# One float32 matmul per product in place of three fp32r matmuls, in a hybrid encoder block on one core

## The chip, the core and the metric

One core of a Trainium2 chip runs the whole block in one launch. The metric is the device time of one execution in microseconds. TensorE (PE) multiplies, with its weight loads shown apart (PEld); VectorE (DVE), ScalarE (ACT) and GpSimd (POOL) work beside it; SyncE (SP) issues most DMAs. Weights and activations are float32 in memory and must come out with float32 accuracy.

## The reference, cut to what matters

```python
x = x + 0.5 * swiglu(rms_norm(x, ffn1_norm), w_gate1, w_up1, w_down1)     # 2048 -> 5504 -> 2048
proj = rms_norm(x, mix_norm) @ w_in                                       # 2048 -> 11280
(gq, gk, gv, gz, ga, gb, aq, ak, av, gate_gdn, gate_att) = split(proj)
o_gdn = gdn_branch(gq, gk, gv, gz, ga, gb, ...)     # conv, chunked gated delta rule, 8 heads of 128
o_att = chunk_attention_branch(aq, ak, av, ...)     # banded softmax attention, 8 heads of 128
m = sigmoid(gate_gdn) * (o_gdn @ w_branch_gdn) + sigmoid(gate_att) * (o_att @ w_branch_att)
x = x + m @ w_out
x = x + 0.5 * swiglu(rms_norm(x, ffn2_norm), w_gate2, w_up2, w_down2)
```

There are 256 tokens, batch 1, one layer, all in float32. Nearly all work is in the large matrix products: 256 tokens times some 100 million weights, read once.

## The kernel before, in words

**Tiles.** The 256 tokens are two halves of 128. An activation block is a 128 x 128 tile (128 features on the partitions, 128 tokens), held as the stationary operand; the weights are the moving operand, up to 512 columns wide, and a result bank is 128 tokens x 512 columns in PSUM. There are 4 result banks of the kind `acc` and 4 of the kind `core`.

**Three matmuls per product.** Every operand of a large product is split in two numbers that TensorE takes in the type fp32r: the high part is the value cast to fp32r (ScalarE), the low part is the value less the high part (VectorE). `product` (lines 507 to 509) adds high x high, high x low and low x high into the same bank. Activations are split by `Xr.plain`, `Xr.more`, `split_to` and `bank_sums`, weights by `split` and `prepare`.

**Seven products in place of eight.** For chosen pairs of k tiles and pairs of column groups (`fast` pairs, in `seven`) the 2 x 2 blocks are multiplied by Winograd's form of Strassen's scheme: seven products of 128 x 128 times 128 x 512 in place of eight. The weights' four sums (`s`, lines 430 to 432) are made on VectorE, and the activations' sums by `act_sums`. The products go to eight banks, whose contents are put together on VectorE and ScalarE (lines 593 to 597, 610). Other pairs use eight plain products. Lists such as `FAST`, `FOUR`, `MIX`, `DOWN`, `DEEP` and `LAST` say which pairs are fast in which product.

**The weights' way.** `plan` lists all weight items in the order of use: one item is two DMAs of 512 KB, a pair of k tiles for two column groups. `load` issues the DMAs of an item to a tile `raw` on SyncE, `split` makes the casts and sums, `prepare` the low halves, and `take_weights` hands the parts to the products. `LOAD` = 2 items are loaded ahead of the one being split, `PREP` = 5 products or rows are ready ahead of TensorE. All of these tiles are in a pool `heap` of 22 buffers of 8 KB per partition. A plain item uses three of them (`raw`, `wh`, `wl`), a fast one five (`raw`, `s`, `w`, `sh`, `sl`) and a half-size one (`v`).

**Order of the work.** The first FFN, the input projections, attention woven with the projections for the gated delta rule (`weave`), the delta rule woven with branch and gate products, the merge, the output product and the second FFN follow each other. `after(n, f)` puts small work n weight items later; `issue_after` places chosen instructions behind others in the order of issue. The second FFN ends in `seven(..., late=...)`, where the last pair's products alternate with the transposes of finished output parts (`store`), and the last column group is transposed and stored after it.

**Other matmuls.** 163 small matmuls (attention scores and values, the delta rule) take plain float32 operands already, at 8 to 256 columns, and 501 are transposes of 128 x 128 tiles; the change leaves them as they are.

Of the kernel before, what the change touches and what calls it, by code (L numbers as in the profile page):

```python
# [12 lines left out]
F32R = mybir.dt.float32r  # L13
# [23 lines left out]
TAIL = {"1": ((0, 1, 2, 3, 4, 5), (0, 1, 5, 3, 4, 2)), "2": ((0, 1, 2, 3, 4, 5), (0, 1, 5, 3, 4, 2))}  # L37
APART = (0, 1, 2, 4, 3, 7, 5, 6)
FIRST = (1, 0, 3, 2, 5, 4, 7, 6)
QUAD = {2: (0, 0), 3: (1, 0), 4: (0, 1), 8: (1, 1)}  # L40
STAND = (3, 4, 6, 7)
CHUNKS = ((0, 4), (4, 8), (8, 11))
# [5 lines left out]
def block_kernel(ctx: ExitStack, tc: tile.TileContext, a: dict, out: bass.AP):  # L48
# [26 lines left out]

    def f32(ap):
        return ap.bitcast(F32)
# [54 lines left out]
    def split_to(hi, lo, src):  # L132
        nc.scalar.copy(hi, src)
        nc.vector.tensor_sub(lo, src, f32(hi))  # L134
# [20 lines left out]
    class Xr:  # L155
# [4 lines left out]
        def __init__(self, nm, wi, fast=()):  # L160
            self.nm, self.wi, self.fast = nm, wi, fast
            self.blk, self.half = {}, None
            self.acc = sp.tile([P, 2, 4], F32, name=f"ssq{nm}", tag="ssq", bufs=2)
            self.rn = sp.tile([P, 2], F32, name=f"rn{nm}", tag="rn", bufs=2)
            self.half_rn = sp.tile([P, 2], F32, name=f"rh{nm}", tag="rh", bufs=2)

        def place(self, j):
            if j in self.fast:
                self.blk[j] = heap([P, 2, 8, P], F32R, f"xf{self.nm}_{j}")
            elif self.half is None:  # L170
                self.half = heap([P, 2, 2, 4, P], F32R, f"xr{self.nm}_{j}")
                self.blk[j] = self.half[:, 0]
            else:
                self.blk[j], self.half = self.half[:, 1], None
            return self.blk[j]
# [4 lines left out]
        def plain(self, j, src, later=None):  # L180

            b = self.place(j)
            for i in range(2):
                hi, lo = (b[:, s, 2 * i : 2 * i + 2, :].rearrange("p t x -> p (t x)") for s in range(2))
                nc.scalar.activation(hi, src(i), AF.Copy, scale=self.w(j, i))
                low = lambda i=i, hi=hi, lo=lo: nc.vector.scalar_tensor_tensor(
                    lo, src(i), self.w(j, i), f32(hi), op0=ALU.mult, op1=ALU.subtract
                )
                later.append(low) if later is not None else low()

        def scale(self, j, src, a):
            for i in range(2):
                nc.scalar.activation(
                    a[:, 2 * i : 2 * i + 2, :].rearrange("p t x -> p (t x)"), src(i), AF.Copy, scale=self.w(j, i)
                )

        def more(self, j, src, blocks=slice(4, 8)):

            a, s = (wide(f"x{x}{self.nm}{j}").rearrange("p (b x) -> p b x", x=P) for x in "as")
            self.scale(j, src, a)  # L200
            act_sums([a[:, b] for b in range(4)], s)
            for b, v in ((0, a), (4, s)):
                if b >= blocks.start:
                    split_to(self.blk[j][:, 0, b : b + 4], self.blk[j][:, 1, b : b + 4], v)

        def add(self, j, src):
            if j in self.fast:
                self.place(j)
                self.more(j, src, slice(0, 8))
            else:  # L210
                self.plain(j, src)
# [20 lines left out]
        def sums_of(self, j, i):  # L232
            return [self.blk[j][:, s, i] for s in range(2)]

        def more_again(self, pairs):

            sums = {}
            for i, j in enumerate(pairs):
                if i % 2 == 0:
                    tile = heap([P, 2, 2, 4, P], F32R, f"xm{self.nm}{j}_{taken[0]}")  # L240
                sums[j] = tile[:, i % 2]

            def make(j):
                a, s = (wide(f"m{x}{self.nm}{j}").rearrange("p (b x) -> p b x", x=P) for x in "as")
                nc.vector.tensor_add(a, f32(self.blk[j][:, 0]), f32(self.blk[j][:, 1]))
                act_sums([a[:, b] for b in range(4)], s)
                split_to(sums[j][:, 0], sums[j][:, 1], s)

            for i, j in enumerate(pairs):
                after(2 + 2 * i, lambda j=j: make(j))  # L250
            return lambda j, b: self.sums_of(j, b) if b < 4 else [sums[j][:, s, b - 4] for s in range(2)]
# [4 lines left out]
    def quads(blk):  # L256
        return lambda k, t: [blk[k // 4][:, k % 4, s, t * P : (t + 1) * P] for s in range(2)]
# [59 lines left out]
    def mixing():  # L317
# [16 lines left out]
        yield from sevens(*gates[0:2])  # L334
        yield from sevens(*gates[2:4])
# [7 lines left out]
    PREP, LOAD = 5, 2  # L343
# [30 lines left out]
    def begin():  # L374
# [5 lines left out]
        with ExitStack() as order:  # L380
            for ins in copied:
                order.enter_context(tc.issue_after(ins))
            if loaded[0][0] - 1 in range(1, 8):
                order.enter_context(tc.issue_after(casts[loaded[0][0] - 1].ins))
            split(*loaded.popleft())
            copied.clear()

    def split(i, fast, pieces, raw):

        if i in (2, 3, 5, 6, 7, 8):  # L390
            j = FIRST[i if i < 4 else i - 1]
            xr1.plain(j, pair_of_x(j), lows)
        if not fast:
            out = []
            ms = [n * kk * (P if len(src.shape) == 3 else 1) for src, n, kk in pieces]
            cuts = [(slice(0, 2), ms[0])] if ms[0] == ms[1] else [(slice(at, at + 1), m) for at, m in enumerate(ms)]
            hl = [heap([P, 2, 1024], F32R, f"w{x}{i}") for x in "hl"]
            if i < 4:
                cuts = [(slice(at, at + 1), m) for at, m in enumerate(ms)]
            todo = [tuple(w[:, at, :m] for w in (*hl, raw)) for at, m in cuts]  # L400
            if i < 2:
                todo = [tuple(by_k(w[:, at], k) for w in (*hl, raw)) for at in range(2) for k in range(2)]
            for hi, _, src in todo:
                casts[i] = nc.scalar.copy(hi, src)  # L404
            for at, (src, n, kk) in enumerate(pieces):
                if len(src.shape) == 3:
                    n *= P
                    cols = [w[:, at, : ms[at]].rearrange("p (c k x) -> p c k x", k=kk, x=P) for w in hl]
                    cols = [[w[:, :, j, :] for j in range(kk)] for w in cols]
                else:  # L410
                    cols = [[w[:, at, j * n : (j + 1) * n] for j in range(kk)] for w in hl]
                out.append((1, (*cols, n), i))
            begun.append((todo, out))
# [4 lines left out]
        w1 = heap([P, 2, 2 * n], F32R, f"w{i}")  # L418
        w2 = half_tile([P, 2, n], F32R, f"v{i}")

        def by_row(w):

            if tiled:
                return w.rearrange("p b (c k x) -> p b k c x", k=2, x=P)
            return w.rearrange("p b (k n) -> p b k n", k=2)

        col = lambda w: w.rearrange("p (c x) -> p c x", x=P) if tiled else w
        R = by_row(raw[:, :, : 2 * n])
        S = s.rearrange("p b (c x) -> p b c x", x=P) if tiled else s
# [7 lines left out]
        casts[i] = nc.scalar.copy(sh, s)  # L437
        parts.append((sh, sl, s))
        k = by_row(w1)
        w11, w21 = ([k[:, s, b] for s in range(2)] for b in range(2))  # L440
        t1, t3, t2, t4 = ((sh[:, b], sl[:, b]) for b in range(4))
        w22 = (w2[:, 0], w2[:, 1])

        prods = ((1, 0, w11), (2, 2, w21), (6, 5, t2), (7, 6, t3), (4, 3, t4), (5, 4, t1), (3, 7, w22))
        if i == 8:
            prods = [prods[at] for at in (0, 2, 3, 5, 1, 4, 6)]
        begun.append((parts, [(4, prods, i)]))

    begun, casts, subs, lows, copied = deque(), {}, {}, deque(), []
    taken = [0]  # L450

    def prepare():
# [5 lines left out]
        todo, out = begun.popleft()  # L458
        for hi, lo, src in todo:
            last = subs[out[0][2]] = nc.vector.tensor_sub(lo, src, f32(hi))  # L460
        if lows:
            with tc.issue_after(last.ins):
                while lows:
                    lows.popleft()()
        ready.extend(out)
# [3 lines left out]
    def take_weights():  # L469
# [4 lines left out]
        _, piece, now[0] = ready.popleft()  # L474
        return piece

    now = [0]

    def behind_next():

        order = ExitStack()
        for found in (casts, subs):
            if now[0] + 1 in found:
# [952 lines left out]
```

## Time and profile before

| what | value |
|---|---|
| time, median of 3 runs | 2090.52 us (2089.24 to 2095.28) |
| the profiled execution | 2090.2 us, of which the profile's span is 2088.4 us |
| TensorE busy, matmuls | 2078.9 us, 9686 |
| VectorE busy | 1886.9 us |
| ScalarE busy | 1225.5 us |
| DMA: read, mean rate | 407.72 MB, 209 GB/s |

The span runs from the first to the last instruction that the profiler recorded. An engine's busy time is the time in which at least one of its instructions ran; matmuls overlap, since the next one starts while the last one drains, so TensorE's speed is read from the distance between their starts. In the group rows the columns are line, engine, operation, output<-inputs, shapes and count, then busy time and mean length of one, then the idle time of the engine before them and who ended it.

### The profile page before, as it was taken

Reading aid. Unit: us, or ns where it says so; the run is one execution under the profiler, and the core shown is the slowest. Engines: PE = TensorE matmul, PEld = TensorE weight load, DVE = VectorE, ACT = ScalarE, POOL = GpSimd, SP = SyncE. Lnnn points to the kernel's source line nnn. Section 1 sums busy time; section 2 is a strip of 40 time slices with the busy share of each in tenths; the row PEclk is TensorE's granted clock in tenths of the full one; section 3 lists DMA queues with packets and bytes.
Section 4 is the critical chain, followed back from the end, with each engine's and each line's share of the span. In section 5 each row is a group of like instructions: output and inputs, shape, how many; then the busy total and the mean of one; then the engine's idle time right before and its main releaser. Section 6 shows DMA issues by size and latency. Waiting matters only on the chain. (4 is left out here: it accounts for less than half of the span.)

```text
span 2088.4 us, 25852 instructions
## 1 busy us (share of the span) xinstructions
PE 2078.9 (100%) x9686; PEld 1733.8 (83%) x9686; DVE 1886.9 (90%) x2145; ACT 1225.5 (59%) x1276; POOL 78.9 (4%) x93
## 2 busy tenths in 40 slices
PE   9999999999999999999999999999999999999999
PEld 7788888888898988888888888888888888888897
DVE  7998999989998989977884887999989999899998
ACT  7755665646555756767654554566555655556554
POOL 0000110002001000000010000000000200011001
PEclk9999999999999999999999999999999999999999
DMA  9655996649868755744554466767655975569567
GB/s 330 223 182 181 254 268 198 206 143 281 257 196 227 267 181 188 235 151 137 186 174 149 157 205 211 234 197 231 209 189 165 289 236 197 181 184 313 184 196 192
DMA packets 401133, 437.74 MB, mean 210 GB/s; under 512 B 14944, under 2 KB 373744, under 8 KB 400752
## 3 DMA queue, kind: packets, MB, share of 16 engines
q1 hardware_dynamic: 389488, 415.12, 61.5%
q0 software_dynamic: 11520, 20.98, 5.8%
q8 instruction: 76, 1.25, 0.3%
q14 instruction: 49, 0.40, 0.1%
HBM read 407.72 MB, written 28.32 MB: 209 GB/s over the span
## 5 line engine op out<-in xcount | busy, mean ns | idle before, releaser
L460 DVE TENSOR_TENSOR wl<-raw,wh 128x2048 fp32r<-128x2048 f32 (+5 forms) x257 | 551.5, 2150 | 49.6 <-ACT wh L404 10.7
L404 ACT CAST wh<-raw 128x2048 fp32r<-128x2048 f32 (+5 forms) x257 | 459.7, 1801 | 88.6 <-DVE wl L460 26.8
L437 ACT CAST sh<-s 128x2048 fp32r<-128x2048 f32 (+1 forms) x139 | 263.7, 1897 | 376.7 <-DVE s L432 358.6
L460 DVE TENSOR_TENSOR sl<-s,sh 128x2048 fp32r<-128x2048 f32 (+1 forms) x139 | 313.8, 2264 | 11.1 <-PE pd L508 3.4
L508 PE MATMUL pf<-wl,xr 128*128 128x512 f32 (+1 forms) x704 | 271.2, 385 | 0.1
L509 PE MATMUL pf<-wh,xr 128*128 128x512 f32 (+1 forms) x704 | 270.7, 384 | 0.0
L507 PE MATMUL pf<-wh,xr 128*128 128x512 f32 (+1 forms) x704 | 264.4, 387 | 0.4 <-DVE ewo L610 0.4
L430 DVE TENSOR_TENSOR s<-raw 128x1024 f32<-128x1024 f32 (+1 forms) x139 | 167.9, 1208 | 20.3 <-PE pd L508 9.3
L435 ACT CAST w<-raw 128x1024 fp32r<-128x1024 f32 (+1 forms) x139 | 144.8, 1042 | 64.0 <-issue 11.8
L460 DVE TENSOR_TENSOR w<-raw,w 128x1024 fp32r<-128x1024 f32 (+1 forms) x139 | 168.0, 1209 | 10.8 <-ACT w L435 10.5
L508 PEld LDWEIGHTS pf<-wl,xr 128*128 128x128 f32 x704 | 132.2, 188 | 26.5 <-DVE wl L460 1.8
L507 PEld LDWEIGHTS pf<-wh,xr 128*128 128x128 f32 x704 | 132.2, 188 | 26.0 <-DVE ewo L610 1.1
L509 PEld LDWEIGHTS pf<-wh,xr 128*128 128x128 f32 x704 | 132.1, 188 | 24.9
L508 PE MATMUL pd<-wl,hid 128*128 128x512 f32 x352 | 138.9, 394 | 0.0
L509 PE MATMUL pd<-wh,hid 128*128 128x512 f32 x352 | 137.7, 391 | 0.0
L697 POOL DMA_DIRECT2D xd<-ed x80 | 69.9, 961 | 1577.5 <-ACT ed L593 1247.6
L507 PE MATMUL pd<-wh,hid 128*128 128x512 f32 x352 | 127.9, 393 | 0.0
L435 ACT CAST v<-raw 128x512 fp32r<-128x512 f32 (+1 forms) x139 | 85.7, 616 | 57.5 <-PE pf L509 35.3
L508 PE MATMUL pf<-sl,xf 128*128 128x512 f32 (+1 forms) x292 | 112.3, 385 | 0.0
L509 PE MATMUL pf<-sh,xf 128*128 128x512 f32 (+1 forms) x292 | 112.0, 385 | 0.0
L507 PE MATMUL pf<-sh,xf 128*128 128x512 f32 (+1 forms) x292 | 110.9, 387 | 1.0 <-DVE hid L134 0.8
L460 DVE TENSOR_TENSOR v<-raw,v 128x512 fp32r<-128x512 f32 (+1 forms) x139 | 94.4, 679 | 1.8 <-ACT v L435 1.8
(550 smaller groups left out, 4397.5 us busy)
## 6 DMA issues: line engine op xcount, KB each, us to landing
raw<-wd SPq DMA_DIRECT2D x168, 512.0 KB, 5.1
raw<-wg SPq DMA_DIRECT2D x158, 512.0 KB, 4.0
raw<-wu SPq DMA_DIRECT2D x158, 512.0 KB, 5.3
raw<-wgt SPq DMA_DIRECT2D x64, 512.0 KB, 4.7
raw<-wa SPq DMA_DIRECT2D x48, 512.0 KB, 4.5
raw<-wc SPq DMA_DIRECT2D x48, 512.0 KB, 4.7
xd<-ed POOLq DMA_DIRECT2D x80, 256.0 KB, 6.9
raw<-wbr SPq DMA_DIRECT2D x32, 512.0 KB, 4.7
```

The lines of the kernel that those rows point to most:

```text
L404: casts[i] = nc.scalar.copy(hi, src)
L430: nc.vector.tensor_sub(S[:, 0:2], R[:, 1], R[:, :, 0])
L435: nc.scalar.copy(hi, src)
L437: casts[i] = nc.scalar.copy(sh, s)
L460: last = subs[out[0][2]] = nc.vector.tensor_sub(lo, src, f32(hi))
L507: nc.tensor.matmul(dst, ah, wh, start=start, stop=False)
L508: nc.tensor.matmul(dst, ah, wl, start=False, stop=False)
L509: return nc.tensor.matmul(dst, al, wh, start=False, stop=stop)
L697: b: lambda e, dst=xd[d + dd][t]: nc.gpsimd.dma_start(dst, e, accum_op=ALU.add)
```

## The change

`product` becomes one matmul of the float32 operands as they are. The tiles of high and low halves go: weights are used straight from `raw`, block sums straight from `s`, activations from one float32 copy. `split` keeps the three VectorE instructions that make the sums of a fast item and nothing else. The helpers that placed casts in the order of issue (`casts`, `subs`, `lows`, `behind_next`) go with them. `LOAD` rises from 2 to 4 (the loads run two items further ahead). Activation sums are made from the copied float32 tile and packed 16 blocks to a buffer (`Blocks`). The order of the seven products of a fast item changes, the fast pairs of two gate/up groups of the first FFN change (4 and 3 pairs become 2 and 4), the first gate of the merge uses 4 fast pairs in place of 3, in the order `GATE`. At the end of the second FFN and of the output product the last items' products are taken bank by bank, and the last output group is transposed and stored by halves of the tokens.

```diff
-    PREP, LOAD = 5, 2
+    PREP, LOAD = 5, 4
...
     def product(dst, act, wt, start, stop):
 
-        (ah, al), (wh, wl) = act, wt
-        dst = dst[:, : int(np.prod(wh.shape[1:]))]
-        if len(wh.shape) == 3:
+        dst = dst[:, : int(np.prod(wt.shape[1:]))]
+        if len(wt.shape) == 3:
             dst = dst.rearrange("p (c x) -> p c x", x=P)
-        nc.tensor.matmul(dst, ah, wh, start=start, stop=False)
-        nc.tensor.matmul(dst, ah, wl, start=False, stop=False)
-        return nc.tensor.matmul(dst, al, wh, start=False, stop=stop)
+        return nc.tensor.matmul(dst, act, wt, start=start, stop=stop)
...
     def split(i, fast, pieces, raw):
...
         nc.vector.tensor_sub(S[:, 0:2], R[:, 1], R[:, :, 0])
         nc.vector.tensor_add(S[:, 2], S[:, 1], R[:, 0, 0])
         nc.vector.tensor_sub(S[:, 3], R[:, 0, 1], S[:, 2])
-        parts = [(w1[:, 0], w1[:, 1], raw[:, 0, : 2 * n]), (col(w2[:, 0]), col(w2[:, 1]), R[:, 1, 1])]
-        for hi, lo, src in parts:
-            nc.scalar.copy(hi, src)
-        sh, sl = (heap([P, 4, n], F32R, f"s{x}{i}") for x in "hl")
-        casts[i] = nc.scalar.copy(sh, s)
-        parts.append((sh, sl, s))
...
-        prods = ((1, 0, w11), (2, 2, w21), (6, 5, t2), (7, 6, t3), (4, 3, t4), (5, 4, t1), (3, 7, w22))
+        w11, w21, w22 = R[:, 0, 0], R[:, 0, 1], R[:, 1, 1]
+        t1, t3, t2, t4 = (s[:, b] for b in range(4))
+
+        prods = ((1, 0, w11), (2, 2, w21), (3, 7, w22), (6, 5, t2), (7, 6, t3), (4, 3, t4), (5, 4, t1))
...
     def prepare():
...
-        todo, out = begun.popleft()
-        for hi, lo, src in todo:
-            last = subs[out[0][2]] = nc.vector.tensor_sub(lo, src, f32(hi))
...
-        ready.extend(out)
+        ready.extend(begun.popleft())
...
-    def split_to(hi, lo, src):
-        nc.scalar.copy(hi, src)
-        nc.vector.tensor_sub(lo, src, f32(hi))
+    class Blocks:
...
+        def take(self, n):
+            if self.at + n > 16:
+                self.tile, self.at = heap([P, 16, P], F32, f"{self.name}_{taken[0]}_{self.at}"), 0
+            self.at += n
+            return self.tile[:, self.at - n : self.at]
...
+        if (f, i) in BY_GROUP:
+            return BY_GROUP[f, i]
...
-            ev = seven(f"g0{d}", 512, DOWN, act)
+            ev = seven(f"g0{d}", 512, MIX, act, pairs=GATE)
...
     def store(d, xs):
         room = heap([P, 4, T], F32, f"y{d}")
+        if d == 3:
+            halves = [core_bank(f"yt{d}{t}") for t in range(2)]
+            for t, ps in enumerate(halves):
+                for c in range(4):
+                    nc.tensor.transpose(ps[:, c * P : (c + 1) * P], xs[t][:, c * P : (c + 1) * P], ident)
+                ps = ps.rearrange("p (c x) -> p c x", c=4)
+                ts = slice(t * P, (t + 1) * P)
+                (nc.vector.tensor_copy if t else nc.scalar.copy)(room[:, :, ts], ps)
+                nc.sync.dma_start(out[:, 4 * d : 4 * d + 4, ts], room[:, :, ts])
+            return
```

How it moves instructions, at three places. On TensorE, the first fast item of the third gate/up group of the first FFN (`pf_8_b` is bank b of that group, `w`, `v` the split weight blocks, `sh` and `sl` the halves of their sums, `xf` and `xr` the activation blocks). Before:

```order
L507 MATMUL pf_8_1_941<-w_816,xf_0_145 128x512
L508 MATMUL pf_8_1_941<-w_816,xf_0_145 128x512
L509 MATMUL pf_8_1_941<-w_816,xf_0_145 128x512
L507 MATMUL pf_8_2_945<-w_816,xf_0_145 128x512
L508 MATMUL pf_8_2_945<-w_816,xf_0_145 128x512
L509 MATMUL pf_8_2_945<-w_816,xf_0_145 128x512
L507 MATMUL pf_8_6_949<-sh_823,xf_0_145 128x512
L508 MATMUL pf_8_6_949<-sl_824,xf_0_145 128x512
L509 MATMUL pf_8_6_949<-sh_823,xf_0_145 128x512
```

After, the whole item:

```order
L434 MATMUL pf_8_1_523<-raw_412,xr_0_16_122 128x512
L434 MATMUL pf_8_2_525<-raw_412,xr_0_16_122 128x512
L434 MATMUL pf_8_3_527<-raw_412,xr_0_16_122 128x512
L434 MATMUL pf_8_6_529<-s_466,xr_0_16_122 128x512
L434 MATMUL pf_8_7_531<-s_466,xr_0_16_122 128x512
L434 MATMUL pf_8_4_533<-s_466,xr_0_16_122 128x512
L434 MATMUL pf_8_5_535<-s_466,xr_0_16_122 128x512
```

Seven instructions stand where 21 stood, they read `raw` and `s` themselves, and the product into bank 3 moved from the end of the item ahead of those of the sums. Over the program TensorE has 2949 products of three matmuls before (2731 of 512 columns, 122 of 384, 64 of 352, 32 of 336) and 2948 of one after (2730 of 512 columns, the others alike).

On VectorE, weight items of the same FFN a little later, between the gate/up results of one group (L632, in the changed kernel L570) and those of the next. Before:

```order
L460 TENSOR_TENSOR w_894<-raw_812,w_894 128x1024
L460 TENSOR_TENSOR v_895<-raw_812,v_895 128x512
L460 TENSOR_TENSOR sl_902<-s_893,sh_901 128x2048
L430 TENSOR_TENSOR s_993<-raw_890 128x1024
L460 TENSOR_TENSOR w_994<-raw_890,w_994 128x1024
L431 TENSOR_TENSOR s_993<-s_993,raw_890 128x512
L460 TENSOR_TENSOR v_995<-raw_890,v_995 128x512
L432 TENSOR_TENSOR s_993<-raw_890,s_993 128x512
L460 TENSOR_TENSOR wl_973<-raw_869,wh_972 128x2048
L460 TENSOR_TENSOR sl_1002<-s_993,sh_1001 128x2048
```

After:

```order
L385 TENSOR_TENSOR s_598<-raw_544 128x1024
L386 TENSOR_TENSOR s_598<-s_598,raw_544 128x512
L387 TENSOR_TENSOR s_598<-raw_544,s_598 128x512
L385 TENSOR_TENSOR s_632<-raw_570 128x1024
L386 TENSOR_TENSOR s_632<-s_632,raw_570 128x512
L387 TENSOR_TENSOR s_632<-raw_570,s_632 128x512
L532 TENSOR_TENSOR ef_8_1_614<-pf_8_6_529,ef_8_0_613 128x512
```

The low halves (L460) are gone and the sums of the items follow each other directly.

On SyncE, in the first gate/up group: the loads of the items 7 on (`raw`, from the gate weights `wg` and the up weights `wu`), the constants and the first stores of the residual stream (`xd`). Before:

```order
L363 DMA raw_252<-wu 128x4x256
L89 DMA xT_81<-x 128x512
L363 DMA raw_287<-wg 128x4x256
L363 DMA raw_287<-wu 128x4x256
L728 DMA xd_82<-xs_311 128x512
L728 DMA xd_83<-xs_312 128x512
L363 DMA raw_343<-wg 128x4x256
L363 DMA raw_343<-wu 128x4x256
```

After:

```order
L343 DMA raw_163<-wu 128x4x256
L87 DMA xT_81<-x 128x512
L343 DMA raw_177<-wg 128x4x256
L343 DMA raw_177<-wu 128x4x256
L343 DMA raw_184<-wg 128x4x256
L343 DMA raw_184<-wu 128x4x256
L351 DMA cst<-cst 128x640
L343 DMA raw_195<-wg 128x4x256
L343 DMA raw_195<-wu 128x4x256
L664 DMA xd_82<-xs_208 128x512
L664 DMA xd_83<-xs_209 128x512
```

Two more items (`raw_184` and `raw_195`) are issued ahead of the first two stores.

More of the change, by code (lines that the diff above doesn't have):

```diff
@@ L167, in place @@
         def place(self, j):
[L168 to L174, printed above, removed]
+            self.blk[j] = self.room.take(8 if j in self.fast else 4)
             return self.blk[j]
@@ L178, in w, with plain, more @@
             return vcol(V_N[self.wi] + 2 * j + i)
-        def plain(self, j, src, later=None):
+        def plain(self, j, src):
             b = self.place(j)
             for i in range(2):
[L184 to L187, printed above, removed]
-                )
[L189 to L204, printed above, removed]
+                nc.scalar.activation(
+                    b[:, 2 * i : 2 * i + 2].rearrange("p t x -> p (t x)"), src(i), AF.Copy, scale=self.w(j, i)
+                )
+        def more(self, j):
+            b = self.blk[j]
+            act_sums([b[:, i] for i in range(4)], b[:, 4:8])
         def add(self, j, src):
+            self.plain(j, src)
             if j in self.fast:
[L208 to L211, printed above, removed]
+                self.more(j)
         def turn(self, g, xs):
@@ L232, in sums_of @@
         def sums_of(self, j, i):
-            return [self.blk[j][:, s, i] for s in range(2)]
+            return self.blk[j][:, i]
         def more_again(self, pairs):
[L237 to L241, printed above, removed]
+            room = Blocks(f"xm{self.nm}")
+            sums = {j: room.take(4) for j in pairs}
             def make(j):
[L244 to L247, printed above, removed]
+                act_sums([self.blk[j][:, i] for i in range(4)], sums[j])
             for i, j in enumerate(pairs):
                 after(2 + 2 * i, lambda j=j: make(j))
-            return lambda j, b: self.sums_of(j, b) if b < 4 else [sums[j][:, s, b - 4] for s in range(2)]
+            return lambda j, b: self.sums_of(j, b) if b < 4 else sums[j][:, b - 4]
         def st(self, k, t):
@@ L333, in mixing @@
             yield from twos(p)
-        yield from sevens(*gates[0:2])
-        yield from sevens(*gates[2:4])
+        for d in (0, 2):
+            yield from sevens(*(t_pieces(a["wgt"], 4 * (d + i), 4, 0, KD, [2 * j for j in GATE]) for i in range(2)), MIX, GATE)
         for d in range(4):
@@ L379, in begin @@
         left[0] -= 1
[L380 to L386, printed above, removed]
+        split(*loaded.popleft())
     def split(i, fast, pieces, raw):
-        if i in (2, 3, 5, 6, 7, 8):
-            j = FIRST[i if i < 4 else i - 1]
-            xr1.plain(j, pair_of_x(j), lows)
         if not fast:
             out = []
[L395 to L404, printed above, removed]
             for at, (src, n, kk) in enumerate(pieces):
@@ L473, in take_weights @@
         taken[0] += 1
[L474 to L483, printed above, removed]
-                order.enter_context(tc.issue_after(found[now[0] + 1].ins))
-        return order
+        return ready.popleft()[1]
     def run(gen):
@@ L640, in gate_up, with block_sums @@
         return us
-    def bank_sums(ps, more, nm):
-        s = wide(f"s{nm}").rearrange("p (b x) -> p b x", x=P)
+    def block_sums(ps, more):
         b = ps.rearrange("p c (t x) -> p (c t) x", x=P)
-        nc.scalar.copy(s[:, 2], b[:, 1])
-        act_sums([b[:, 0], s[:, 2], b[:, 2], b[:, 3]], s)
-        split_to(more[:, 0], more[:, 1], s)
+        act_sums([b[:, i] for i in range(4)], more)
     def residual(d, nm):
@@ L664, in ffn, with hidden @@
         jobs = deque()
-        def hidden(hb, us, m, c0, more):
-            for c, mm, ps in turn(lambda t: us[t][:, c0 * P :], min(2, m - c0), f"{hb.name}_{c0}"):
+        def hidden(hn, hb, us, m, c0, more):
+            for c, mm, ps in turn(lambda t: us[t][:, c0 * P :], min(2, m - c0), f"{hn}_{c0}"):
                 dst = hb[:, c0 : c0 + mm]
-                split_to(dst[:, :, 0, :], dst[:, :, 1, :], ps)
+                nc.scalar.copy(dst, ps)
                 if more is not None:
-                    bank_sums(ps, more, f"{hb.name}_{c0}")
+                    block_sums(dst, more)
         for a0, a1 in CHUNKS:
-            hid, fast, sums, half = [], down_pairs(f, a1), {}, None
+            hid, fast, sums, room = [], down_pairs(f, a1), {}, Blocks(f"hs{nm}_{a0}")
             for i in range(a0, a1):
@@ L683, in ffn @@
                     if j in fast:
-                        half = heap([P, 2, 2, 4, P], F32R, f"hs{nm}_{i}{j}") if half is None else half
-                        sums[j], half = (half[:, 0], half) if len(sums) % 2 == 0 else (half[:, 1], None)
-                    jobs.append(lambda hb=hb, us=us, m=m, c0=c0, s=sums.get(j): hidden(hb, us, m, c0, s))
+                        sums[j] = room.take(4)
+                    jobs.append(lambda hn=f"hid{nm}_{i}", hb=hb, us=us, m=m, c0=c0, s=sums.get(j): hidden(hn, hb, us, m, c0, s))
             n = 3
@@ L692, in ffn @@
             act = quads(hid)
-            block = lambda j, b: act(2 * j + b // 2, b % 2) if b < 4 else [sums[j][:, s, b - 4] for s in range(2)]
+            block = lambda j, b: act(2 * j + b // 2, b % 2) if b < 4 else sums[j][:, b - 4]
             kt = sum(FG[a1 - 1]) - FG[a0][0]
@@ L1240, in block_kernel @@
     xr1.plain(FIRST[0], pair_of_x(FIRST[0]))
-    def more(s):
-        xr1.more(FIRST[s], pair_of_x(FIRST[s]))
     def feed(s):
-        if s == 0:
-            with tc.issue_after(casts[0].ins):
-                xr1.plain(FIRST[1], pair_of_x(FIRST[1]))
         if s == 8:
             nc.sync.dma_start(hd, a["hd"].partition_broadcast(P))
-            after(2, lambda: more(7))
             after(4, xr1.finish)
             return
-        if s > 1 and FIRST[s - 1] in xr1.fast:
-            with tc.issue_after(casts[s + 1].ins):
-                more(s - 1)
+        if s < 7:
+            xr1.plain(FIRST[s + 1], pair_of_x(FIRST[s + 1]))
+        if FIRST[s] in xr1.fast:
+            xr1.more(FIRST[s])
         for k4 in range(4):
@@ L1283, in branch_att @@
             yield from gemm_steps(pss, H, quads(ob), 512)
[L1284 to L1286 removed]
+            for t in range(2):
+                nc.scalar.copy(G1[t][:, 512 * d : 512 * (d + 1)], pss[t])
             yield
```

145 lines of the change are left out of this document (74 added, 71 removed).

## The prediction

> **What bounds the kernel now.** I read the page's busy times first, then the groups with their waits, then the engine table over long stretches, and last the timeline of TensorE around the few matmuls that are already plain float32. The page:
>
> ```profile
> span 2088.4 us, 25852 instructions
> PE 2078.9 (100%) x9686; PEld 1733.8 (83%) x9686; DVE 1886.9 (90%) x2145; ACT 1225.5 (59%) x1276; POOL 78.9 (4%) x93
> ...
> PEclk9999999999999999999999999999999999999999
> ...
> HBM read 407.72 MB, written 28.32 MB: 209 GB/s over the span
> ```
>
> TensorE is busy for the whole span at full clock, VectorE is close behind, and the DMA engines have room. Since busy matmuls overlap, what counts is their pitch, start to start. The table of engines by stretch, for TensorE alone (length, busy time, matmuls begun):
>
> ```profile
> 743.60:869.60 126.00, 126.00 (x557) 1.00 0.65 213
> 1663.00:1736.90 73.90, 73.90 (x327) 1.00 0.76 239
> ...
> 40.00:2040.00 2000.00, 1997.74 (x9324) 1.00 0.67 208
> ```
>
> Two stretches of nothing but 512-column fp32r matmuls, one in the mixing part and one in the second FFN, give 126.0/556 = 0.2266 us and 73.9/326 = 0.2267 us each: no engine keeps TensorE waiting there. Between 40 and 2040 us it is idle for 2.3 us. So VectorE and ScalarE, however full, are not on the path.
>
> The narrower products, from the timeline (start, length): 352 columns (12 pitches between the two rows) and 384 columns (5 pitches).
>
> ```profile
> 709.99 0.32 PE L509 MATMUL pav<-wh,xr 128*128 128x352 f32 x1
> ...
> 711.91 0.32 PE L509 MATMUL pav<-wh,xr 128*128 128x352 f32 x1
> ```
> ```profile
> 603.11 0.33 PE L508 MATMUL pf<-sl,xf 128*128 128x384 f32 x1
> ...
> 603.98 0.33 PE L507 MATMUL pf<-sh,xf 128*128 128x384 f32 x1
> ```
>
> 1.92/12 = 0.160 us and 0.87/5 = 0.174 us. From 352 to 512 columns the pitch rises by 66.6 ns, 0.416 ns a column, so an fp32r matmul takes 0.416 ns per column plus 13.5 ns (336 columns, used in a few: 0.1533 us).
>
> **The price of a float32 matmul.** The kernel holds 163 of them, all narrow. Groups by shape (count, busy, mean length), then two places of the timeline:
>
> ```profile
> L825 PE MATMUL as<-att_kT,att_qT 128*128 128x256 f32 x16 | 4.1, 378 | 0.0
> L825 PE MATMUL as<-att_kT,att_qT 128*128 128x128 f32 x16 | 2.1, 274 | 0.0
> L1105 PE MATMUL pd<-gdn_ls,gdn_pk 128*128 128x32 f32 x32 | 3.7, 270 | 0.0
> ```
> ```profile
> 965.12 0.39 PE L509 MATMUL pc<-wh,xr 128*128 128x512 f32 x1
> 965.35 1.02 PE L825 MATMUL as<-att_kT,att_qT 128*128 128x256 f32 x4
> 966.02 0.58 PE L507 MATMUL pc<-wh,xr 128*128 128x512 f32 x1
> ```
> ```profile
> 927.28 1.05 PE L825 MATMUL as<-att_kT,att_qT 128*128 128x128 f32 x8
> ```
>
> L825 issues 8 matmuls of 256 columns and 8 of 128, and each width has 16 records: one float32 matmul is two records. The four records at 965.35 last 1.02 us together and 0.378 us each, so their pitch is (1.02 - 0.378)/3 = 0.214 us; the eight at 927.28 give (1.05 - 0.274)/7 = 0.111 us. A 256-column record thus costs 214 ns, just two fp32r streams of 256 columns (2 x 256 x 0.416 = 213 ns) with almost no fixed part. 128 columns sit near a floor: 32 columns last as long as 128 (270 against 274 ns). So a float32 product streams four times, an fp32r one once.
>
> No 512-column float32 record is in the trace. Its lower bound is the straight line through 128 and 256 columns: 214 + 2 x 103 = 420 ns. Its upper bound adds the 13.5 ns of an fp32r matmul to two streams of 512: 426 + 13.5 = 440 ns. I take 428 ns, twice the 256-column record, the nearest row. A lower price than three fp32r matmuls is not shut out by a row of that width; it is rival (c).
>
> **The change part by part.**
>
> The products. By the order of instructions TensorE issues 2731 products of 512 columns, 122 of 384, 64 of 352 and 32 of 336, three matmuls each. By the rates above: 3 x (2731 x 0.2266 + 122 x 0.174 + 64 x 0.160 + 32 x 0.1533) = 1856.5 + 63.7 + 30.7 + 14.7 = 1966 us. Now there are 2730, 122, 64 and 32 (one more pair of k tiles goes by seven products in place of eight), two records each of 428, 321, 294 and 281 ns: 2336.9 + 78.3 + 37.6 + 18.0 = 2471 us. That is 505 us more, all on the path, since TensorE never waits for long. Both schemes load 128x128 weights for every record; a load lasts 188 ns, hidden behind 428 as behind 227.
>
> ```profile
> L508 PEld LDWEIGHTS pf<-wl,xr 128*128 128x128 f32 x704 | 132.2, 188 | 26.5 <-DVE wl L460 1.8
> ```
>
> The casts and low halves:
>
> ```profile
> L460 DVE TENSOR_TENSOR wl<-raw,wh 128x2048 fp32r<-128x2048 f32 (+5 forms) x257 | 551.5, 2150 | 49.6 <-ACT wh L404 10.7
> L404 ACT CAST wh<-raw 128x2048 fp32r<-128x2048 f32 (+5 forms) x257 | 459.7, 1801 | 88.6 <-DVE wl L460 26.8
> L437 ACT CAST sh<-s 128x2048 fp32r<-128x2048 f32 (+1 forms) x139 | 263.7, 1897 | 376.7 <-DVE s L432 358.6
> L460 DVE TENSOR_TENSOR sl<-s,sh 128x2048 fp32r<-128x2048 f32 (+1 forms) x139 | 313.8, 2264 | 11.1 <-PE pd L508 3.4
> ```
>
> These four go, 865 us of VectorE and 723 us of ScalarE, with the smaller splits of the same lines. They lie beside TensorE work, so their removal is worth nothing but the waits they cause. The sums of weight blocks stay on VectorE.
>
> The waits. The rest of the span is 2088.4 - 1966 = 122 us. Of it:
>
> ```profile
> 6.02 0.82 PE L507 MATMUL pf<-wh,xr 128*128 128x512 f32 x1
> ```
> ```profile
> 2082.07 0.39 PE L509 MATMUL pd<-wh,hid 128*128 128x512 f32 x1
> ```
> ```profile
> PE xs L1231 <- ACT xs L1232: 0.9, 1, 0.9
> PE pf L507 <- DVE hid L134: 0.8, 1, 0.8
> ```
>
> 6.0 us pass before the first product and 6.3 us from the last one to the end. The page counts 9686 matmuls; without 8847 of products and 12 that only warm the array, 827 transposes and small matmuls remain, 0.11 us each, 91 us. That leaves about 20 us of short waits, the longest listed being 0.9 us. An operand now needs fewer steps on VectorE and ScalarE and each product lasts longer, so I give back 11 us of them, between nothing and all 20.
>
> Loads two items further ahead. A weight item (two loads of 512 KB) feeds 7 or 8 products, so it is now used up in 7 x 0.856 = 6.0 us or more; a load lands sooner after its issue (KB, median us to landing):
>
> ```profile
> raw<-wg SPq DMA_DIRECT2D x158, 512.0 KB, 4.0
> ```
>
> 408 MB over 2.58 ms is 158 GB/s against 209 now, so earlier issue buys nothing and costs nothing; what it is moved ahead of on SyncE (early stores of the stream) is not waited for by TensorE. A raw tile now stays until its last product has read it, but two tiles of high and low halves an item are gone, so buffers are not short. The other order at the end, the last store in halves of the tokens, touches the 6.3 us tail: within 1.5 us, taken as nothing. Block sums made from copied tiles, and other pairs chosen for seven products, hide behind VectorE's freed time.
>
> The sum: 2471 + 122 - 11 = 2582 us of span. The profiled execution took 2090.2 us for a span of 2088.4, 0.3 us under the median of 2090.52, so I add 1.8 and 0.3: 2584 us, slower by 24%.
>
> **Rivals.**
>
> (a) Each float32 record pays the fixed 13.5 ns too. For it: every fp32r width pays it. Against it: the 256-column record has 1 ns. Price: 5896 records x 12 ns = 71 us, 2655 us.
>
> (b) Weights come late. For it: a raw tile is held for longer, and TensorE would queue behind the slowest load. Against it: the DMA demand falls by a quarter. If each of some 390 items (408 MB by 1.05 MB) cost 0.2 us, 78 us: 2662 us.
>
> (c) The one on the other side: two records of a single stream. A float32 product would then cost two fp32r matmuls in place of three: 1966 x 2/3 = 1311 us, with the rest (122 - 11 + 2) 1424 us; DMA would need 408 MB / 1424 us = 287 GB/s, which three slices of the page reach:
>
> ```profile
> GB/s 330 223 182 181 254 268 198 206 143 281 257 196 227 267 181 188 235 151 137 186 174 149 157 205 211 234 197 231 209 189 165 289 236 197 181 184 313 184 196 192
> ```
>
> For it: only that no wide record has been seen. Against it: 214 ns at 256 columns, where one stream with its fixed part would be 120. It decides for "faster" as soon as a 512-column record takes under 340 ns, half of three times 226.6.
> The Trainium skill, Perfetto Trace Analysis, section Engine Utilization, puts the array's output rate at half for the low/high form of float32. Read as the rate of a whole product, that makes an estimate of 427 ns a product and some 1345 us in all; read as the rate of each record it gives 427 ns a record, and there the trace agrees with its 214 ns for 256 columns.
>
> (d) Nothing moves, because VectorE (90% busy) was the real limit and the longer products fill its waits. Against it: the two dense stretches without a wait. It would need TensorE to have 500 us to spare; it has about 20.
>
> **How the numbers follow.** The forecast case, 2555 to 2615 us: 0.80. (a) 0.10, (b) 0.06, (c) 0.03, (d) 0.01. The bounds of the record reach from 420 ns (2730 x 2 x 8 ns = 44 us less) to 440 ns; with the waits' bounds of -9 and +11 (not both ends at once) and rival (a) the range is 2540 to 2655 us, which leaves out (c), (d) and some of (b). A measurement here tells about 0.3%. Faster 0.03, same 0.01, slower 0.96.
>
> **What would show it.** On the profile after: TensorE with 9686 - 8847 + 5896 = 6735 records, the products at a pitch near 0.428 us, busy all the time; VectorE down by more than 865 us and ScalarE by more than 723 us without any gain; SyncE's loads landing long before use. Wrong would be a pitch below 0.40 (then (c) or some third rate), a pitch at 0.44 ((a)), or long waits of TensorE for raw weights ((b)).

## The result and the profile after

The changed kernel takes 2586.3 us (median of 4 runs, 2586.1 to 2588.36). The kernel before, run beside it, takes 2092.53 us (2089.24 to 2095.28, 4 runs). The ratio is 1.236, with an interval from 1.234 to 1.239: slower by 24%, as forecast (2584 us).

The page of the kernel after, its busy times and its clock:

```profile
span 2584.5 us, 17569 instructions
PE 2576.7 (100%) x6735; PEld 1210.6 (47%) x6735; DVE 768.1 (30%) x1326; ACT 284.9 (11%) x527; POOL 78.5 (3%) x93
...
PEclk9999999999999999999999999999999999999999
...
HBM read 407.72 MB, written 28.32 MB: 169 GB/s over the span
```

The matmul records fell from 9686 to 6735, VectorE's busy time from 1886.9 to 768.1 us and ScalarE's from 1225.5 to 284.9 us. The clock is full and the DMA engines have less to do per microsecond. TensorE was busy throughout before and still is; only now its work is longer. The freed 1119 us of VectorE and 941 us of ScalarE bought nothing that can be seen on this page.

TensorE's timeline of the kernel after gives the pitch of a 512-column float32 record, a width that the trace of before did not hold (start, length, records; each 512-column product shows as two records):

```profile
592.84 15.61 PE L434 MATMUL pd<-raw,hid 128*128 128x512 f32 x36
608.29 1.02 PE L434 MATMUL pd<-raw,hs 128*128 128x512 f32 x2
```

36 records fill 608.29 - 592.84 = 15.45 us, 0.4292 us each. For 352 columns there is one long row, and the groups by shape give the length of a single record:

```profile
878.61 21.76 PE L434 MATMUL pav<-raw,xr 128*128 128x352 f32 x73
```
```profile
L434 PE MATMUL pf<-raw,xr 128*128 128x512 f32 x1900 | 831.6, 592 | 2.0 <-ACT xr L183 2.0
...
L434 PE MATMUL pav<-raw,xr 128*128 128x352 f32 x128 | 38.2, 459 | 0.0
```

(21.76 - 0.459)/72 = 0.2958 us. So a float32 record costs (429.2 - 295.8)/160 = 0.834 ns a column and 2.2 ns more, which gives 322.5 ns for 384 columns and 282.4 ns for 336; the starts of such records in the trace lie 322.6 and 282.5 ns apart on the mean. A product is two such records.

TensorE over the long middle part (length, busy time, records, granted clock, DMA share, GB/s), and all that it waited for in the whole span (total, times, longest, in us):

```profile
40.00:2540.00 2500.00, 2499.89 (x6522) 1.00 0.54 168
```
```profile
PE pf L434 <- ACT xr L183: 2.0, 1, 2.0
PE idle L93 <- DVE zero L90: 1.2, 1, 1.2
PE yt L677 <- DVE ed L522: 0.3, 1, 0.3
```

In 2500 us TensorE is idle for 0.1 us (2.3 us in 2000 us before). The waits listed are three, 3.5 us in all. One of them is new: at 29 us the first products wait for the activations, which ScalarE makes one after the other behind the squares of the first norm. On ScalarE's timeline they are one row:

```profile
28.92 3.40 ACT L183 ACTIVATE xr<-xT,vec 128x256 f32<-128x256 f32 x8
```

Idle time doesn't show every wait, since a record that starts late can still overlap the one before it. The starts in the two traces show the rest. Behind another product, the records of the kernel before start some 16.0 us later in all than the pitches of their widths add up to; in the kernel after they start on time (-0.2 us). The small matmuls, each group with the step to the product behind it, take 96 us in both; after, that holds the new wait.

### The profile page after: what moved, and what is told of

The parts are those of the page before. It is cut to its first block, busy times and chain, and to the rows that moved or that the text cites. A ratio compares the mean times of both kernels' runs of the same rounds, so it can differ in the third digit from the quotient of the medians.

```text
span 2584.5 us, 17569 instructions
## 1 busy us (share of the span) xinstructions
PE 2576.7 (100%) x6735; PEld 1210.6 (47%) x6735; DVE 768.1 (30%) x1326; ACT 284.9 (11%) x527; POOL 78.5 (3%) x93
## 4 chain that ended last, share of the span: by engine, by line
PE 100%; ACT 0%; DVE 0%; issue 0%
PE pf L434 43%; PE pd L434 21%; PE pg L434 8%; PE pc L434 6%; PE pwo L434 4%; PE pav L434 2%; PE pz L434 2%; PE pwb L434 2%; PE pwa L434 2%; PE pak L434 2%; PE paq L434 2%; PE hid L148 1%; PE pd L1051 0%; PE xt L148 0%; PE ao L802 0%; PE ct L148 0%
## 5 line engine op out<-in xcount | busy, mean ns | idle before, releaser
L434 PE MATMUL pf<-raw,xr 128*128 128x512 f32 (+1 forms) x2096 | 896.8, 582 | 2.0 <-ACT xr L183 2.0
L434 PEld LDWEIGHTS pf<-raw,xr 128*128 128x128 f32 x2096 | 395.7, 190 | 469.0 <-issue 437.7
L434 PE MATMUL pd<-raw,hid 128*128 128x512 f32 x872 | 384.2, 592 | 0.0
L434 PEld LDWEIGHTS pd<-raw,hid 128*128 128x128 f32 x872 | 164.7, 190 | 201.9 <-issue 200.2
L434 PE MATMUL pf<-s,xr 128*128 128x512 f32 (+1 forms) x576 | 254.0, 583 | 0.0
L434 PE MATMUL pg<-raw,xr 128*128 128x512 f32 x416 | 181.7, 593 | 0.0
L434 PEld LDWEIGHTS pf<-s,xr 128*128 128x128 f32 x576 | 109.4, 190 | 132.6 <-issue 123.2
L434 PE MATMUL pc<-raw,xr 128*128 128x512 f32 x336 | 147.7, 592 | 0.0
L434 PE MATMUL pd<-s,hs 128*128 128x512 f32 x252 | 122.2, 592 | 0.0
L387 DVE TENSOR_TENSOR s<-raw,s 128x512 f32<-128x512 f32 (+1 forms) x140 | 95.9, 686 | 4.2
```

Of the source, the lines that this page charges most:

```text
L387: nc.vector.tensor_sub(S[:, 3], R[:, 0, 1], S[:, 2])
L434: return nc.tensor.matmul(dst, act, wt, start=start, stop=stop)
```

## Experiments: what a float32 record costs

All experiments were timed beside the kernel before.

**Four fp32r matmuls against one float32.** The kernel before, with the fourth term (low half by low half) added, so that TensorE does as many streams for a product as the float32 matmul is thought to do:

```
-        return nc.tensor.matmul(dst, al, wh, start=False, stop=stop)
+        nc.tensor.matmul(dst, al, wh, start=False, stop=False)
+        return nc.tensor.matmul(dst, al, wl, start=False, stop=stop)
```

> The kernel before with a fourth fp32r matmul per product (low x low), so that a product streams four times as a float32 one does. Theory (a matmul costs its streams plus a fixed part, and fp32r pays 13.5 ns for each matmul where a float32 record pays 2.6): 2949 more matmuls of 226.6 ns (174, 160 and 153 for the narrow ones) add 655 us, 2748 us (2735 to 2760), about 160 us over the changed kernel. Rival 1 (four streams cost the same in whatever form): 2586 us. Rival 2 (VectorE is the real limit and the longer products fill its waits): well below 2700 us.

Measured: 2733.76 us (2733.62 to 2733.88, 4 runs), a ratio of 1.307 (1.305 to 1.309). The page of this kernel and TensorE's row of a stretch of nothing but 512-column products:

```profile
PE 2725.7 (100%) x12635; PEld 2284.9 (84%) x12635; DVE 1927.3 (71%) x2145; ACT 1240.9 (45%) x1276; POOL 78.4 (3%) x93
```
```profile
973.40:1136.30 162.90, 162.90 (x720) 1.00 0.49 161
```

162.9/719 = 0.2266 us, as in the kernel before. The time is 1 us under the low end of what was expected. Short waits vanished here too: late starts behind another product, counted as above, sum to 5.4 us where the kernel before has 16.0. Four fp32r matmuls take 4 x 226.6 = 906 ns and one float32 matmul 2 x 429.2 = 858 ns. The difference is 48 ns a product of 512 columns and, by the rates of each width, 48 to 51 ns a narrower one: 142 us over the 2948 products, of the 147 us between the two kernels. So by its time the float32 matmul is four streams in two records, with 2 x 2.2 ns of fixed cost in place of 4 x 13.5 ns. (Whether a record streams its columns twice or once at half the rate can't be told from these times, and makes no difference to them.) And the change loses because it trades three streams for four.

The Trainium skill, FP8 and Floating Point Precision, section TensorE Precision Notes, says that true FP32 takes four passes through the array (high and low half by high and low half). The times of these two kernels agree with it.

**The fixed part of a record.** Rival (a) gave each float32 record the 13.5 ns of an fp32r one. If that is so, cutting the records into narrower ones makes them dearer by that much each. In the kernel after, every product but the first of a bank was cut into pieces of 256 columns, in a second kernel into pieces of 128:

```
+        n, step = wt.shape[1], 256 // (P if len(wt.shape) == 3 else 1)
+        for c in range(0, n, step):
+            e = min(c + step, n)
+            last = nc.tensor.matmul(dst[:, c:e], act, wt[:, c:e], start=False, stop=stop and e == n)
```

> The changed kernel with every product but the first of a bank issued as pieces of 256 columns. Theory (a 256-column record costs 215 ns, half of a 512-column one): 1.4 ns more per product, with the narrow ones 10 us more, 2597 us. Rival (each piece hands over at a fixed cost of 13.5 ns as fp32r does): 2 records x 2 pieces x 11 ns x 2400 products, over 2680 us.

> The changed kernel with every product but the first of a bank issued as pieces of 128 columns (10042 pieces in place of 2582 matmuls, the same streams). Theory (a float32 record of 128 columns sits at a floor of 111.5 ns, so four pieces cost 892 ns against 859): 33 ns more for 2386 products, with the narrow ones 90 us more, 2676 us. Rival (only the streams and 2.6 ns per record count): 14 ns more per product, about 2620 us. Rival (pieces cost nothing): 2586 us.

Measured: 2606.01 us with 256 columns (2 runs, ratio 1.246, 1.244 to 1.249), 2680.38 us with 128 (2 runs, ratio 1.282, 1.279 to 1.284). The timelines of the two, first 256 and then 128 columns:

```profile
2450.16 9.66 PE L439 MATMUL pf<-raw,xr 128*128 128x256 f32 x44
2459.65 3.62 PE L439 MATMUL pf<-s,xr 128*128 128x256 f32 x16
```
```profile
2521.12 9.99 PE L439 MATMUL pf<-raw,xr 128*128 128x128 f32 x88
2530.95 3.74 PE L439 MATMUL pf<-s,xr 128*128 128x128 f32 x32
```

9.49/44 = 0.2157 us and 9.83/88 = 0.1117 us: 2 x 215.7 = 431.4 ns and 4 x 111.7 = 446.8 ns where an uncut record takes 429.2. The forecast of the 128-column kernel holds (4 us off). The 256-column one came out 9 us above its own forecast: its pieces have a mean pitch of 216.2 ns over 9516 pairs of neighbours in the trace, 1.6 ns above half an uncut record (214.6 ns), where the 215 ns of the forecast allowed 0.4. The page of that kernel has 11899 records in place of 6735. At 13.5 ns for each of the 5164 records that the cut adds, it would have cost 70 us; it cost 20. Rival (a) falls.

**The same fixed part in bf16.** Is the small fixed part special to float32, or the large one to fp32r? The bf16 matmuls that warm the array at the start, 60 in place of 12 (one run, 2594.22 us):

> The changed kernel with 60 in place of 12 warming matmuls (bf16, 512 columns, zeros) at its start, to see their pitch at full clock. Theory (the fixed 13.5 ns belongs to fp32r, not to every matmul): 213 to 217 ns each, some 10 us more in all. Rival (it is the hand-over of weights that any single matmul pays): 226 ns.

Two views of their timeline, one 10 records longer than the other, and TensorE's row there with the clock:

```profile
6.79 5.56 PE L93 MATMUL idle<-zero 128*128 128x512 bf16 x25
```
```profile
6.79 7.72 PE L93 MATMUL idle<-zero 128*128 128x512 bf16 x35
```
```profile
6.90:14.00 7.10, 7.10 (x35) 1.00 1.12 322
```

(7.72 - 5.56)/10 = 0.216 us at full clock, 3 ns above 512 x 0.416 = 213 ns. So the 13.5 ns belong to fp32r. The Trainium skill, TensorE: Matmul & The Clock Gate, section on the HAM clock gate, has N / 2.4 GHz and about 2.5 ns, 215.7 ns, for a warm matmul of 512 columns; this run agrees. Beside it a float32 record takes 429.2/216 = 1.99 times as long.

## Experiments: where VectorE, ScalarE and the loads stand

**The casts put back.** Rival (d) held VectorE to be the limit. In the kernel after, ScalarE again casts weights and block sums to fp32r and VectorE again makes their low halves; nothing reads them:

```
+            hi, lo = (heap([P, 2, 1024], F32R, f"d{x}{i}") for x in "hl")
...
+                nc.scalar.copy(hi[:, at, :m], raw[:, at, :m])
+                nc.vector.tensor_sub(lo[:, at, :m], raw[:, at, :m], hi[:, at, :m].bitcast(F32))
```

> The changed kernel with the weights' casts to fp32r on ScalarE and their low halves on VectorE put back, written and never read; products stay single float32 matmuls. Theory (TensorE's streams set the time, the casts lie beside them): VectorE's busy time near 1900 us and ScalarE's near 1240 us, the time within 0.3% of the changed kernel's 2586 us. Rival (removing the casts was a gain that hides a larger cost of the float32 products): slower than it by 1% or more, 2612 us up.

Measured: 2594.31 us (2594.17 to 2595.1, 4 runs), ratio 1.241 (1.239 to 1.243). With VectorE's busy time back from 768 to 1825 us and ScalarE's from 285 to 1196 us the kernel is 8.0 us slower than the kernel after, 0.31%, a little over the 0.3% expected. Page, TensorE's first wait and ScalarE's timeline at that place:

```profile
PE 2580.3 (99%) x6735; PEld 1211.3 (47%) x6735; DVE 1824.5 (70%) x1994; ACT 1196.4 (46%) x1195; POOL 78.3 (3%) x93
```
```profile
PE pf L449 <- ACT xr L184: 7.3, 1, 7.3
```
```profile
31.00 3.69 ACT L370 CAST dh<-raw 128x2048 fp32r<-128x2048 f32 x2
...
34.59 1.71 ACT L184 ACTIVATE xr<-xT,vec 128x256 f32<-128x256 f32 x4
```

The first activations stand behind two casts on ScalarE, and the wait of 2.0 us grew to 7.3. To see whether that is all, the same casts were made from the 13th weight item on only:

> The casts and low halves put back as in the run before of that kind, but from the thirteenth weight item on, so that ScalarE's queue is free while the first activations are made. Theory (what the casts cost there was one wait for activations at the start, 7.3 us in place of 2.0): 2587 us, within 3 us of the changed kernel's 2586.3, with over 1750 us of VectorE busy. Rival (the 8 us were spread over the whole run, in waits too short to be listed): 2594 us again.

Measured: 2589.59 us (2589.46 to 2590.43, 5 runs), ratio 1.238 (1.237 to 1.240). The page and the wait:

```profile
PE 2579.7 (100%) x6735; PEld 1211.2 (47%) x6735; DVE 1795.6 (69%) x1978; ACT 1171.5 (45%) x1179; POOL 78.6 (3%) x93
```
```profile
PE pf L449 <- ACT xr L184: 2.0, 1, 2.0
```

The wait is back at 2.0 us, and with it 4.7 of the 8.0 us. The other 3.3 us (0.13%) show as busy time of TensorE (2579.7 against 2576.7 us in the kernel after), not as waits. The trace tells where they come from. TensorE's rows of the same 3.5 us behind that wait, the kernel after first, then this one (the fifth number is the granted clock):

```profile
30.50:34.00 3.50, 3.50 (x10) 1.00 1.09 356
```
```profile
30.50:34.00 3.50, 3.50 (x5) 0.51 1.09 355
```

At half the clock 5 records begin where 10 did. Laid beside the trace of the kernel after, record by record, the products of this kernel are 0.7 us late before that wait, 2.4 us late behind this stretch and 3.0 us late at the end. So 0.7 us come from the start, 1.7 us from the clock, and 0.6 us from the 2550 us in which the casts run beside the products; the rest of the 3.3 us lies behind the last product. The first two need no casts: the traced execution of the next experiment, which has none, shows them too. So over 1000 us of VectorE work and almost 900 us of ScalarE work lie beside TensorE at a price of some 0.6 us in the executions that were traced. In the run with all casts the same comparison gives 0.4 us at the start, 5.3 us of longer wait, 2.5 us behind it at a clock of 0.50 and 0.6 us for the rest. Casts cost most at the one place where they stand ahead of something that TensorE needs. Rival (d) falls.

**The loads.** The kernel after with the lead of the loads as before:

```
-    PREP, LOAD = 5, 4
+    PREP, LOAD = 5, 2
```

> The changed kernel with the loads 2 items ahead again, in place of 4. Theory (DMA at 169 GB/s has room and no wait for a weight is on the path): within 0.3% of 2586 us. Rival (the earlier loads hide waits that the kernel would otherwise have): 10 us slower or more.

Measured: 2588.66 us (2586.38 to 2588.84, 4 runs), ratio 1.238 (1.236 to 1.239); the difference to 2586.3 us is 0.09%. The three waits of TensorE read as in the kernel after. The traced execution (2588.84 us) is 0.9 us late from the first products on and loses 1.7 us more at half the clock behind the wait at 30 us; from there to the end, 2545 us, it keeps step with the kernel after to 0.01 us. Rival (b) falls: loads two items later do not make TensorE wait either.

**The small edits.** The kernel after with the choice of the pairs that go by seven products, the order of the gate, the tail of the second FFN and the last store as before:

```
-BY_GROUP = {("1", 1): FAST[:2], ("1", 2): FOUR}
+BY_GROUP = {}
...
-GATE = (1, 3, 0, 2, 5, 4, 6, 7)
+GATE = (0, 1, 2, 3, 4, 5, 6, 7)
...
-        if d == 3:
+        if d == 9:
```

> The changed kernel with its small edits undone: the fast pairs of two gate/up groups and of the first gate, the order of its pairs, the order of the last down product's items, and the last store by column pairs. Theory: one product more and a tail longer by 0 to 1.5 us, 2586 to 2590 us, no change that can be told. Rival (these edits carry part of the kernel's time): over 2594 us.

Measured: 2587.58 us (2587.17 to 2587.86, 5 runs), ratio 1.237 (1.236 to 1.239): 1.3 us, 0.05%. Nothing of the 494 us lies there. The order of the seven products of a fast item and the packing of the block sums were left as in the kernel after.

## Experiments: is there room under the kernel before?

These leave out terms of the products and tell what the other engines would allow, which is also what rival (c) would have met.

**Two fp32r matmuls in place of three.** The kernel before without the high-by-low matmul of low activations (`al` by `wh`); the low halves are all still made:

```
-        nc.tensor.matmul(dst, ah, wl, start=False, stop=False)
-        return nc.tensor.matmul(dst, al, wh, start=False, stop=stop)
+        return nc.tensor.matmul(dst, ah, wl, start=False, stop=stop)
```

> The kernel before without its third matmul (low half of the activations x high half of the weights is left out of each product; the low halves are still made). Theory: TensorE needs 2/3 of 1966 us and about 115, so 1425 us, but VectorE's 1887 us of work now set the time: 1890 to 2000 us, TensorE waiting for weights. Rival (VectorE's work shrinks or overlaps when TensorE is quicker, TensorE still sets the time): 1430 to 1500 us.

Measured: 1999.25 us (1997.39 to 2001.11, 2 runs), ratio 0.956 (0.954 to 0.958). A third of the products' time on TensorE is gone and the kernel is only 4.4% faster. Its page, TensorE over nearly the whole span (length, busy time, records, granted clock), its longest wait, and what that wait's casts waited for:

```profile
PE 1637.0 (82%) x6737; PEld 1248.8 (63%) x6737; DVE 1872.7 (94%) x2145; ACT 1214.0 (61%) x1276; POOL 81.9 (4%) x93
```
```profile
6.00:1990.00 1984.00, 1631.75 (x6719) 0.92 0.70 219
```
```profile
PE pf L507 <- ACT sh L437: 92.7, 49, 3.2
```
```profile
ACT sh L437 <- DVE s L432: 194.3, 85, 6.4
```

VectorE, 94% busy with 1872.7 us, is the limit now (the next experiment bears it out), and TensorE idles for 352 of 1984 us. TensorE waits for the casts of the block sums, which wait for the sums on VectorE, as the last row shows. The kernel before stood some 90 us ahead of a second wall, which one could not see in its time.

**And the weights' low halves left out.** The kernel before without the `wl` matmul and without the low halves of weights and block sums (weights then count only as far as fp32r holds them):

```
-        for hi, lo, src in todo:
-            last = subs[out[0][2]] = nc.vector.tensor_sub(lo, src, f32(hi))
...
-        nc.tensor.matmul(dst, ah, wl, start=False, stop=False)
```

> The kernel before without its middle matmul and without the weights' low halves: each product is two fp32r matmuls, and the weights count only in their fp32r rounding. It stands for the rival of the prediction in which a product costs two streams: TensorE 1311 us and about 110 beside it, VectorE 1128 us lighter. Theory (TensorE's streams set the time as long as no other engine has more): 1423 us, up to 1500 us if ScalarE's 1225 us of casts or the loads at 287 GB/s come into the way. Rival (VectorE's low halves were not what held the two-matmul kernel at 1999 us): over 1800 us.

Measured: 1520.27 us (1519.69 to 1520.86, 2 runs), ratio 0.727 (0.726 to 0.729). VectorE fell to 833.1 us and the wall with it:

```profile
PE 1452.8 (96%) x6737; PEld 1194.4 (79%) x6737; DVE 833.1 (55%) x1471; ACT 1198.4 (79%) x1276; POOL 79.4 (5%) x93
```
```profile
PE pf L504 <- ACT sh L437: 22.5, 14, 2.8
```

It is 20 us above the top of what was expected: TensorE now waits for ScalarE's casts at several places, the longest group 22.5 us. In all it idles for 66 us (10 us in the kernel before), and its granted clock is 0.984 on the mean. Rival (c) has no casts, so those waits would not have held back its 1424 us; that is argued and was not run.

**A cheaper middle matmul.** bf16 takes 216 ns where fp32r takes 226.6, and a low half is small, so 2532 of the middle matmuls were run in bf16, on low halves written in bf16 and against a stationary tile of zeros (the term is thus left out in them):

```
-        nc.tensor.matmul(dst, ah, wl, start=False, stop=False)
+        nc.tensor.matmul(dst, zb if wl.dtype == BF16 else ah, wl, start=False, stop=False)
```

> The kernel before, where 2532 of the 2949 middle matmuls (high half of the activations x low half of the weights) are bf16: the weights' low halves are written as bf16, and the stationary operand is a block of zeros, so that this term is left out there; only its time is looked at. Theory (the extra fixed part belongs to fp32r: a bf16 matmul of 512 columns has a pitch of 216 ns against 226.6): 10.6 ns x 2532 = 27 us less, 2064 us (2058 to 2072). Rival (a change of type between neighbours costs as much as it saves, or the pitch is set by the mix): 2085 us or more.

Measured: 2112.98 us (2111.58 to 2116.53, 4 runs), ratio 1.010 (1.009 to 1.012). This expectation was wrong by 49 us, and the rival, that a change of type costs, holds. TensorE's timeline over one product, the first rows of two products five apart, and the weight loads' waits (fp32r operands are printed as f32):

```profile
760.76 0.40 PE L511 MATMUL paq<-sh,xm 128*128 128x512 f32 x1
761.00 0.39 PE L512 MATMUL paq<-sl,zb 128*128 128x512 bf16 x1
761.04 0.58 PE L513 MATMUL paq<-sh,xm 128*128 128x512 f32 x1
761.46 0.40 PE L511 MATMUL paq<-sh,xr 128*128 128x512 f32 x1
```
```profile
918.08 0.40 PE L511 MATMUL pc<-wh,xr 128*128 128x512 f32 x1
...
921.55 0.39 PE L511 MATMUL pc<-wh,xr 128*128 128x512 f32 x1
```
```profile
PEld L512 <- issue: 625.0, 2383, 0.5
```

The five products take (921.55 - 918.08)/5 = 0.694 us each, against 3 x 0.2267 = 0.680 us: 14 ns more, where 10 ns less were expected. Over the whole trace 1909 such products of 512 columns have a median of 695 ns from start to start, 2270 in the kernel before one of 680 ns. 2532 x 10 ns would be 25 us gained; measured are 20 us lost. The loads for the bf16 matmul stand in wait for nothing that the profile names. The 361 products of 512 columns that stayed in fp32r throughout have a median of 691 ns in this kernel, so the loss is not in the bf16 matmul alone. Whether it is that load or the switch itself that costs was not told apart.

None of these is a complete kernel that beats the kernel before: those that are faster leave out a term of the product.

## Why the prediction was right, point by point

- **The bound.** TensorE carried the span before and carries it after. Shown for the kernel before by the fourth matmul, which adds 655 us of streams and made it 643 us longer, and for the kernel after by the two casts experiments: VectorE and ScalarE at nearly their old load cost 8 us at most.
- **Records.** 6735, as counted from the order of instructions.
- **The price of a 512-column record.** Taken as 428 ns from twice the 256-column row, with bounds of 420 and 440; measured 429.2. Over the four widths the products take 5460 x 0.4292 + 244 x 0.3225 + 128 x 0.2958 + 64 x 0.2824 = 2478 us instead of 2471: this term was 7 us too small.
- **The waits given back.** The rest of the span was put at 122 - 11 = 111 us; it is 2584.5 - 2478 = 106.5 us, so 15 to 16 us went, not 11. This term was 5 us too cautious. The mechanism holds: late starts behind another product went from 16.0 us to nothing, and what the small matmuls and their steps take stayed at 96 us, close to the 91 us put for them. The two errors of 7 and 5 us offset each other by luck, and the agreement to 2 us is closer than the steps deserve. The four-term experiment shows the same from another side: with longer products 11 us of late starts are gone.
- **No gain from VectorE, ScalarE and earlier loads.** Shown, except for the one place at 29 us where the queue on ScalarE does count. The loads took longer to land than before (in the median 5.2 against 4.0 us for the gate weights, 6.3 against 5.3 us for the up weights), and TensorE never waited for them.
- **Rivals.** (a) falls by the pitch and the pieces, (b) by the waits and the later loads, (c) by the pitch of 0.429 us (it needed 0.340), (d) by the 24% and by the casts put back.

## What to carry to other kernels

Price a matmul by its pitch, start to start, in a stretch where nothing waits, and count streams, not instructions: one float32 matmul is two records of two streams each by their time, 858 ns at 512 columns against 680 ns for three fp32r matmuls. Work taken off engines that TensorE didn't wait for bought nothing here, however full they looked. But look there for the next wall: the kernel before was within 5% of VectorE's, and an edit that shortens TensorE's work meets it at once.

## What the runs showed of the hardware that was not expected

- An fp32r matmul has 13.5 ns of fixed cost by the widths measured, a bf16 one and a float32 record 2 to 3 ns at 512 columns: 227 ns for fp32r against 216 for bf16.
- A bf16 matmul between two fp32r matmuls costs some 15 ns more for the three than fp32r alone (695 against 680 ns, median), although it is the cheaper one by itself (216 against 227 ns).
- A 128-column float32 record takes 111.7 ns, 5 ns over its two streams, 256 columns 215.7 to 216.2 ns.
- Where TensorE waits a little at many places (82% busy) the granted clock fell to 0.92 on the mean, as the row of the kernel with two fp32r matmuls shows; in the dense stretches quoted here it stayed at 1.00.
- Behind one wait of 2.0 us the clock fell to half for 3.41 us in the traced executions of two kernels (late casts, later loads) and not in that of the kernel after, which has the same wait: some 1.7 us. One of the other executions of the kernel after took 2588.36 us at a mean clock of 0.999 in place of 1.000. What decides whether the clock falls there is open.
